# Four of eight pairs by seven products, five tiles summed by DMA, in both feed-forwards of a Conformer layer

## The chip, the cores and the metric

The kernel runs on one core of one Trainium2 chip. The metric is the time of one execution on the device in microseconds. Three runs of the kernel before took 2105.33, 2106.32 and 2113.24 us; their median is 2106.32 us. Where the text speaks of faster or slower, it compares such times of both kernels on the same chip.

## The reference, cut to what matters

One layer, 256 tokens of width 2048, all in float32:

```python
h = rms_norm(x, ffn1_norm);  x = x + 0.5 * swiglu_ffn(h, ffn1_w_in, ffn1_w_out)
h = rms_norm(x, mix_norm);   p = h @ w_mix_in        # conv value | conv gate | gMLP u | gMLP v
x = x + concat(rms_norm(conv_group(p)), rms_norm(gating_group(p))) @ w_mix_out
x = x + memory_cross_attention(rms_norm(x, xattn_norm), rms_norm(mem, mem_norm), w_q, w_kv, w_o)
h = rms_norm(x, ffn2_norm);  x = x + 0.5 * swiglu_ffn(h, ffn2_w_in, ffn2_w_out)
return rms_norm(x, final_norm)

def swiglu_ffn(h, w_in, w_out):
    gate, up = jnp.split(h @ w_in, 2, axis=-1)
    return (jax.nn.silu(gate) * up) @ w_out          # w_in 2048 x 11264, w_out 5632 x 2048
```

## The kernel before, in words

**Precision.** Every float32 operand is split into a high part, which is its value rounded to the type float32r, and a low part, the rest. A product of two matrices is three products of such parts: high by high, high by low, low by high. ScalarE makes the high part with a cast (L112 in most stages, L339 in the first half of a feed-forward), VectorE the low part with a subtraction (L113, L340). Weights come from DRAM as tiles of 128 x 1024 (512 KB) on SyncE's queue.

**The first half of a feed-forward** (class `FeedForward`, L299 to L513) computes silu(gate) * up. x lies with features on the partitions (`xT`), 16 tiles k of 128 features by 256 tokens, multiplied by the norm's gain (`gained`), split, and kept as `x_hl`. The inverse root of the mean square comes later, as a factor for each token, in `give`. The columns of `w_in` go in 11 groups of 512 gate and 512 up columns. Group 0 (`run`, the loop over k) is done plainly, 12 products of 128x512 for each k (`by_two`). For groups 1 to 10 the sixteen k go in eight pairs, and a string names how each is done:

- a C pair (`eight`) takes 2 x 12 = 24 products of 128x512;
- an S pair (`seven`) treats the two k tiles and the two token halves as a 2x2 block matrix and needs seven block products in place of eight, 21 products of 128x512. VectorE makes the sums of weight blocks (L388, L389, L394, L401), 512 columns each, and ScalarE and VectorE split four tiles, three of 1024 columns and one of 512. The matching sums of x (`forms`) are made once, by `sides`, during group 0.

The seven results lie in PSUM banks. After the last S pair (`spairs[-1]`) ScalarE copies one bank and VectorE combines it with three others (L439 to L443), which frees them; the C pairs go on adding to four banks, which are added at the group's end (L452), before `give` takes the silu. A group uses all eight banks, so that the next group's first products wait for these steps.

**Summed tiles.** For the k in `SUMMED` no low part is made on VectorE. `summed` has ScalarE write -w, rounded (L358), and the high part (L359) into a buffer of `hls`, and GpSimd's queue issues a DMA that adds w to -w in place (L360), which leaves the low part. When such a tile has been used, the next in order with the same buffer is begun.

**Buffers.** Split tiles go round in a ring: three of pool `whl` and two of `ring`. In the first feed-forward `x_given` adds one more to the ring, and a second buffer to `hls`, in the space of `xT`, since x is not needed in SBUF until the feed-forward's output is added; x is loaded from its input again later (L557 to L559). In the second, x is a result and stays in SBUF, so there is no such room. Weight tiles before the split go round in nine buffers, four of `wraw` and five of spare space.

**The second half** (`gemm_n`) multiplies the transposed result by `w_out`; the transposes (`turn`) run between its steps, the first four in the last group of the first half. In the second feed-forward x is transposed on VectorE (L989) into `x2` at the same time, for the final sum. At the end `add_up` and `give` (L1014 to L1042) make the final norm, first of one half of the tokens, then of the other.

**The start.** x, the vectors `pv` and the weights are loaded by SyncE's queue in program order; `x_squares` loads x a second time, tokens on the partitions, into tiles of `wraw` for the sums of squares.

**Order.** A planner puts each engine's instructions in an order before the run, by its own estimate of when each can start; on the chip each engine follows this order strictly. `issue_after` adds an edge to that order.

## Time and profile before

| | us |
|---|---|
| median of three runs | 2106.32 |
| the profiled execution | 2108.84 |
| its span, first to last instruction | 2107.0 |
| TensorE busy | 2084.5 |
| VectorE busy | 1576.8 |
| ScalarE busy | 1161.6 |

The profiled execution is a run of its own, with 1.84 us around its span. A matmul's busy time in the rows is its time from start to end; products overlap in the pipeline, so that the distance between starts is shorter than the row's duration. "L339" is a line of the kernel's source, "hl<-spare" a written tile and what is read. A row of a timeline has the start, the duration, the engine, the line, the operation, the tiles, the count and, in brackets, the idle time before it and what ended that. A row of groups has busy time, mean duration, idle time before and what ended most of it. The granted clock of TensorE was 0.998 on average.

### The profile page before, as it was taken

How to read it: one execution, taken by the hardware profiler on the slowest of the kernel's cores; microseconds unless marked ns; L12 is line 12 of the kernel's file. 1: busy time of each engine (PE TensorE's matmuls, PEld its weight loads, DVE VectorE, ACT ScalarE, POOL GpSimd, SP SyncE). 2: the span in 40 equal slices, each digit the busy share in tenths (PEclk: the TensorE clock that was granted, in tenths of full speed). 3: DMA queues.
4: the chain of work that ended last, by engine and by line, in shares of the span. 5: the costliest groups of instructions: out<-in, count | busy, mean ns of one | idle time of the engine just before them, and what ended most of it. 6: DMA issues, size and time to landing. Idle time of an engine off the chain costs nothing.

```text
span 2107.0 us, 26590 instructions
## 1 busy us (share of the span) xinstructions
PE 2084.5 (99%) x9764; PEld 1738.5 (83%) x9764; DVE 1576.8 (75%) x2215; ACT 1161.6 (55%) x1450; POOL 67.7 (3%) x83
## 2 busy tenths in 40 slices
PE   8999999999999999999999999999999999999998
PEld 6888888888888888888888888888888888888886
DVE  6888888876655589889877665777888887787754
ACT  7666566645544454445665454556665666554443
POOL 0000000000000000000000000000000000000000
PEclk9999999999999999999999999999999999999999
DMA  9778777855666676666565543686787778556664
GB/s 360 230 227 257 229 238 245 263 167 169 216 198 188 206 236 200 190 176 185 176 201 185 186 154 111 206 281 191 231 259 247 232 229 250 178 160 202 197 192 149
DMA packets 122244, 442.34 MB, mean 210 GB/s; under 512 B 13697, under 2 KB 13825, under 8 KB 121729
## 3 DMA queue, kind: packets, MB, share of 16 engines
q1 hardware_dynamic: 113184, 407.35, 58.8%
q0 software_dynamic: 8640, 32.51, 8.5%
q8 instruction: 76, 1.25, 0.2%
q10 hardware_dynamic: 288, 0.79, 0.1%
q14 instruction: 56, 0.45, 0.1%
HBM read 438.49 MB, written 2.10 MB: 209 GB/s over the span
## 4 chain that ended last, share of the span: by engine, by line
PE 84%; issue 11%; DMA 2%; ACT 1%; POOL 1%; DVE 1%; SPq 0%; POOLq 0%; ACTq 0%
PE acc L172 12%; PE acc L173 12%; PE acc L171 12%; PE acc L125 9%; PE acc L289 7%; PE acc L288 7%; PE acc L291 7%; PE acc L126 4%; PE acc L277 2%; PE acc L276 2%; PE acc L275 2%; PE aux L263 1%; PE acc L1066 1%; PE acc L1065 1%; PE acc L1067 1%
## 5 line engine op out<-in xcount | busy, mean ns | idle before, releaser
L113 DVE TENSOR_TENSOR hl<-raw,hl 128x1024 fp32r<-128x1024 f32 (+1 forms) x402 | 488.6, 1216 | 282.5 <-ACT hl L112 281.1
L112 ACT CAST hl<-raw 128x1024 fp32r<-128x1024 f32 (+1 forms) x402 | 419.7, 1045 | 481.6 <-PE acc L173 289.3
L339 ACT CAST hl<-spare 128x1024 fp32r<-128x1024 f32 (+1 forms) x135 | 131.8, 993 | 95.5 <-DVE spare L389 38.5
L340 DVE TENSOR_TENSOR hl<-spare,hl 128x1024 fp32r<-128x1024 f32 (+1 forms) x135 | 154.4, 1150 | 35.8 <-ACT hl L339 34.2
L288 PE MATMUL acc<-hl,x_hl 128*128 128x512 f32 x408 | 144.2, 394 | 9.7 <-ACT hl L339 9.7
L289 PE MATMUL acc<-hl,x_hl 128*128 128x512 f32 x408 | 149.9, 395 | 0.0
L340 DVE TENSOR_TENSOR hl<-raw,hl 128x1024 fp32r<-128x1024 f32 (+1 forms) x101 | 113.9, 1131 | 45.9 <-ACT hl L339 44.3
L339 ACT CAST ring<-spare 128x1024 fp32r<-128x1024 f32 (+1 forms) x99 | 97.2, 988 | 68.9 <-DVE spare L389 26.9
L340 DVE TENSOR_TENSOR ring<-spare,ring 128x1024 fp32r<-128x1024 f32 (+1 forms) x99 | 112.9, 1145 | 19.9 <-ACT ring L339 18.8
L291 PE MATMUL acc<-hl,x_hl 128*128 128x512 f32 x408 | 127.5, 392 | 0.0
L339 ACT CAST hl<-raw 128x1024 fp32r<-128x1024 f32 (+1 forms) x101 | 97.7, 977 | 51.8 <-PE acc L291 16.1
L172 PE MATMUL acc<-hl,x_hl 128*128 128x512 f32 x256 | 100.5, 392 | 0.2 <-DVE hl L113 0.2
L172 PE MATMUL acc<-hl,m_hl 128*128 128x512 f32 x256 | 100.4, 392 | 0.0
L173 PE MATMUL acc<-hl,m_hl 128*128 128x512 f32 x256 | 100.2, 391 | 0.0
L173 PE MATMUL acc<-hl,x_hl 128*128 128x512 f32 x256 | 99.8, 390 | 0.0
L288 PEld LDWEIGHTS acc<-hl,x_hl 128*128 128x128 f32 x408 | 76.8, 189 | 25.9 <-ACT hl L339 10.1
L289 PE MATMUL acc<-ring,x_hl 128*128 128x512 f32 x248 | 93.1, 389 | 0.0
L288 PE MATMUL acc<-ring,x_hl 128*128 128x512 f32 x248 | 91.2, 390 | 0.0
L171 PE MATMUL acc<-hl,m_hl 128*128 128x512 f32 x256 | 91.2, 393 | 0.0
L289 PEld LDWEIGHTS acc<-hl,x_hl 128*128 128x128 f32 x408 | 77.2, 190 | 16.9 <-DVE hl L340 1.1
L291 PEld LDWEIGHTS acc<-hl,x_hl 128*128 128x128 f32 x408 | 77.5, 190 | 16.4
L125 PE MATMUL acc<-x_hl,hl 128*128 128x512 f32 x256 | 91.0, 398 | 0.0
(359 smaller groups left out, 5173.9 us busy)
## 6 DMA issues: line engine op xcount, KB each, us to landing
spare<-in_ffn_w_in SPq DMA_DIRECT2D x192, 512.0 KB, 6.4
raw<-in_ffn_w_out SPq DMA_DIRECT2D x176, 512.0 KB, 3.8
raw<-in_ffn_w_in SPq DMA_DIRECT2D x160, 512.0 KB, 6.3
hl_s<-in_ffn_w_in POOLq DMA_DIRECT2D x44, 512.0 KB, 7.3
raw<-in_w_mix_vg SPq DMA_DIRECT2D x32, 512.0 KB, 4.6
raw<-in_w_k SPq DMA_DIRECT2D x32, 512.0 KB, 4.0
raw<-in_w_v SPq DMA_DIRECT2D x32, 512.0 KB, 4.4
raw<-in_w_mix_out SPq DMA_DIRECT2D x32, 512.0 KB, 4.6
```

Of the source, the lines that this page charges most:

```text
L112: nc.scalar.copy(out=hl[:, 0, :size], in_=raw[:, :size])
L113: newest[0] = nc.vector.tensor_tensor(out=hl[:, 1, :size], in0=raw[:, :size], in1=hl[:, 0, :size].bitcast(F32), op=ALU.subtract)
L125: nc.tensor.matmul(acc, lhsT=w_hi, rhs=x_hl, start=first, stop=False, skip_group_check=True)
L126: nc.tensor.matmul(acc[:, 0], lhsT=w_lo, rhs=x_hl[:, 0], start=False, stop=last, skip_group_check=True)
L171: nc.tensor.matmul(acc[t], lhsT=x[:, 0, s], rhs=hi[:, k], start=k0 + k == 0, stop=False)
L172: nc.tensor.matmul(acc[t], lhsT=x[:, 0, s], rhs=lo[:, k], start=False, stop=False)
L173: nc.tensor.matmul(acc[t], lhsT=x[:, 1, s], rhs=hi[:, k], start=False, stop=k0 + k == nk - 1)
L288: nc.tensor.matmul(acc[t][g], lhsT=x[:, 0, s], rhs=hi[:, cols[g]], start=(t, g) in first, stop=False)
L289: nc.tensor.matmul(acc[t][g], lhsT=x[:, 0, s], rhs=lo[:, cols[g]], start=False, stop=False)
L291: nc.tensor.matmul(acc[t][g], lhsT=x[:, 1, s], rhs=hi[:, cols[g]], start=False, stop=last)
L339: nc.scalar.copy(out=hl[:, 0, :n], in_=raw[:, :n])
L340: newest[0] = nc.vector.tensor_tensor(out=hl[:, 1, :n], in0=raw[:, :n], in1=hl[:, 0, :n].bitcast(F32), op=ALU.subtract)
```

## The change

- **Pairs.** Pair 6 turns from C to S in both patterns. The summed k go from 2, 7, 13 to 2, 6, 7, 11, 14. `sides` makes a fourth set of sums of x, at k = 15 of group 0. Two transposes rather than four run in the last group of the first half.
- **Space of x.** In the second feed-forward the residual x is stored to a DRAM tile (`kept`) while the attention's output product makes it, by four DMAs on GpSimd's queue; `x_given` then takes its space as in the first feed-forward, and `x_back` loads it again after the last group.
- **Head.** Gains and the first tile of x come as one transfer on ScalarE's queue, the second tile of x behind it. Eleven products of a tile of ones run on TensorE ahead of the first real one. The first weight tile comes and is split in two halves (`early`). The loads of x for the squares go to tiles of `h`, not `wraw`, and are asked for at k = 2, 4, 6, 8, not 5, 7, 9, 11. `give` of group 0 comes ahead of the second summed tile.
- **End.** Of the four partial sums of squares of the final norm, the first three are added, scaled and given the epsilon ahead of the last product (`most`); the last one goes directly into the square root. One operation with two factors from memory becomes a `tensor_scalar`.

```diff
-PATTERNS = ("SCSCSCCC", "SCSCSCCC")
-SUMMED = ((2, 7, 13), (2, 7, 13))
+PATTERNS = ("SCSCSCSC", "SCSCSCSC")
+SUMMED = ((2, 6, 7, 11, 14), (2, 6, 7, 11, 14))
+WARM = 11
...
-    xT = xt.tile([P, KD, T], F32, name="xT", tag="x")
+    gx = xt.tile([P, KD + KD * T], F32, name="gx", tag="x")
+    gains, xT = gx[:, :KD], gx[:, KD:].rearrange("p (k t) -> p k t", t=T)
+    nc.scalar.dma_start(out=gx[:, :KD + T], in_=a["gains_x0"])
+    nc.scalar.dma_start(out=xT[:, 1], in_=a["xT"][:, 1])
+    nc.vector.memset(ones, 1.0)
+    idle = pa.tile([P, 2, T], F32, name="aux")
+    for _ in range(WARM):
+        nc.tensor.matmul(idle[:, 0, :P], lhsT=ones, rhs=ones, start=True, stop=True)
...
+    def x_given():
+        more = xt.tile([P, 4, 1024], F32R, name="more", tag="x")
+        ff.ring.append(more[:, :2])
+        ff.hls.append(more[:, 2:])
+
+    def x_back(src):
+        xT = xt.tile([P, KD, T], F32, name="xT", tag="x")
+        for k in range(0, KD, 8):
+            nc.gpsimd.dma_start(out=xT[:, k:k + 8], in_=src[:, k:k + 8])
+        return xT
...
                     late = p > self.spairs[-1] and len(after) > 0
                     self.eight(j, p, b, p == self.pattern.index("C"), p == n - 1, late)
-                    if p > self.spairs[-1] + 1:
+                    if p >= n - 2:
...
+        def early(self, before):
+            self.raw_at += 1
+            self.at += 1
+            raw = wraw.tile([P, 1024], F32, name="raw")
+            hl = whl.tile([P, 2, 1024], F32R, name="hl")
+            halves = [slice(G, 2 * G), slice(0, G)]
+            for s in halves:
+                nc.sync.dma_start(out=raw[:, s], in_=self.w_in[0, :, 0, s])
+            x = before(0)
+            for s in halves:
+                with tc.issue_after(x.ins):
+                    split(hl[:, 0, s], hl[:, 1, s], raw[:, s])
+            return hl
...
+            self.give(0, [acc[t][0] for t in range(2)], [acc[t][1] for t in range(2)], r)
             if more is not None:
                 more()
                 self.summed(1)
-            self.give(0, [acc[t][0] for t in range(2)], [acc[t][1] for t in range(2)], r)
...
-                    now, turns = turns[:4], turns[4:]
+                    at = 2 * self.pattern[-2:].count("C")
+                    now, turns = turns[:at], turns[at:]
...
     def x_squares(c):
-        raw = wraw.tile([P, 1024], F32, name="raw")
+        raw = ff.h[7 - c].rearrange("p a b -> p (a b)")
...
-            if k in (5, 7, 9, 11):
-                x_squares(k // 2 - 2)
-            if k in (6, 9, 12):
+            if k in (2, 4, 6, 8):
+                x_squares(k // 2 - 1)
+            if k in (6, 9, 12, 15):
                 ff.sides(k // 3 - 2)
...
+            kept = tc.dram_tile([P, KD, T], F32, name="kept")
             for f in range(KD):
...
                 residual(acc, f, 1.0, x_hl, "ffn2_norm", ss)
+                if f % 4 == 3:
+                    nc.gpsimd.dma_start(out=kept[:, f - 3:f + 1], in_=xT[:, f - 3:f + 1])
...
-        turns = ff.run(lambda k: None, first_beside, lambda: rms_cols(ss, D, "r_x2"))
+        turns = ff.run(lambda k: None, first_beside, lambda: rms_cols(ss, D, "r_x2"), x_given)
+        xT = x_back(kept)
...
-            nc.vector.reduce_sum(out=tot, in_=sums[:, t], axis=AX.X)
-            nc.scalar.activation(out=s, in_=tot, func=AF.Sqrt, scale=1.0 / D, bias=eps)
-            nc.vector.tensor_scalar(out=v, in0=tot, scalar1=1.0 / D, scalar2=RMS_EPS, op0=ALU.mult, op1=ALU.add)
+            last = sums[:, t, 3:4]
+            nc.scalar.activation(out=s, in_=last, func=AF.Sqrt, scale=1.0 / D, bias=most[t])
+            nc.vector.tensor_scalar(out=v, in0=last, scalar1=1.0 / D, scalar2=most[t], op0=ALU.mult, op1=ALU.add)
             nc.vector.reciprocal(out=r, in_=s)
-            nc.vector.scalar_tensor_tensor(out=r, in0=v, scalar=r, in1=s, op0=ALU.mult, op1=ALU.add)
+            nc.vector.tensor_scalar(out=r, in0=v, scalar1=r, scalar2=s, op0=ALU.mult, op1=ALU.add)
...
+        most = [st.tile([P, 1], F32, name=f"f_most{t}") for t in range(2)]
+        for t in range(2):
+            nc.vector.reduce_sum(out=most[t], in_=sums[:, t, 0:3], axis=AX.X)
+            nc.vector.tensor_scalar(
+                out=most[t], in0=most[t], scalar1=1.0 / D, scalar2=RMS_EPS, op0=ALU.mult, op1=ALU.add
+            )
```

51 lines of the change are left out of this document (22 added, 29 removed).

## The prediction

> **What bounds the kernel now.** I read the page first, then the busy time of stretches, then single engines in order of time. The page's head, its busy line and the queue of GpSimd's transfers:
>
> ```profile
> span 2107.0 us, 26590 instructions
> PE 2084.5 (99%) x9764; PEld 1738.5 (83%) x9764; DVE 1576.8 (75%) x2215; ACT 1161.6 (55%) x1450; POOL 67.7 (3%) x83
> q0 software_dynamic: 8640, 32.51, 8.5%
> ```
>
> TensorE is busy in 99% of the span, so a product that goes away shortens the run, unless TensorE then waits for something. Stretches next: the start, the stretch after a late wait at 44.8, and one of about a column group in each feed-forward (busy time and count by engine, granted clock, DMA share, GB/s):
>
> ```profile
> core 0: us, PE busy (x) PEld busy (x) DVE busy (x) ACT busy (x) POOL busy (x), PEclk, DMA share, GB/s
> 7.10:12.00 4.90, 4.89 (x13) 3.89 (x14) 4.41 (x6) 3.83 (x6) 0.00 (x0) 1.00 1.02 369
> 44.80:49.40 4.60, 4.58 (x13) 3.34 (x14) 3.65 (x7) 2.40 (x3) 0.00 (x0) 0.63 1.04 315
> 101.00:143.00 42.00, 42.00 (x187) 34.80 (x186) 34.98 (x43) 25.59 (x30) 2.60 (x3) 1.00 0.75 241
> 1524.00:1566.00 42.00, 42.00 (x187) 34.80 (x186) 35.89 (x45) 26.48 (x29) 2.60 (x3) 1.00 0.79 239
> ```
>
> Inside the groups TensorE never rests, VectorE is busy 83 to 85%, ScalarE 61 to 63%, the DMA engines 75 to 79%. VectorE and the DMA engines are what the change can push to the edge.
>
> **The products.** TensorE's pitch, from product starts in one seven-product pair of the second feed-forward:
>
> ```profile
> 1524.37 0.39 PE L275 MATMUL acc<-ring 128*128 128x512 f32 x1
> ...
> 1526.86 0.39 PE L277 MATMUL acc<-hl,x_hl 128*128 128x512 f32 x1
> ```
>
> Eleven products lie between these starts: 2.49 / 11 = 0.226 us each. A C pair issues 24 of them, an S pair 21. One of eight pairs turns from C to S in ten groups of two feed-forwards: 20 x 3 = 60 products, **-13.6 us**. A group goes from 183 products, 41.4 us, to 180, 40.8 us.
>
> What this asks of the other engines, from the groups of instructions of the first feed-forward (us busy, mean ns | idle before):
>
> ```profile
> L340 DVE TENSOR_TENSOR hl<-spare,hl 128x1024 fp32r<-128x1024 f32 x48 | 58.2, 1222 | 8.0 <-ACT hl L339 7.4
> L388 DVE TENSOR_TENSOR spare<-spare 128x512 f32<-128x512 f32 x16 | 11.0, 686 | 10.1 <-DMA spare<-in_ffn_w_in 10.1
> L339 ACT CAST hl<-raw 128x1024 fp32r<-128x1024 f32 x33 | 34.4, 1050 | 8.2 <-PE acc L291 4.5 <-issue 1.4 <-PE aux L277 1.2
> ```
>
> VectorE: an S pair costs three wide splits and five half-wide operations, 3 x 1.22 + 5 x 0.69 = 7.1 us. Gone are the splits of k 12, 6, 11 and 14 (13 was summed already), 4 x 1.22 = 4.9. Net +2.2 on about 34.5 a group: 36.7 of 40.8, 90%. ScalarE: three wide casts and a half one (estimated 0.6) in, four casts out, two more summed tiles in, with two passes each, as long as a cast: +3.8 on 25.7, 72%. DMA: 8.5% of the span is 179 us for 8640 packets, or 2.65 for the 128 packets of a 512 KB tile, and five rather than three such tiles a group: +5.3 on 0.77 x 41.4 = 31.9, which makes 37.2 of 40.8, **91%**. None is over 100%, so none of them sets the pace by its sum; a wait must come from a latency or a burst.
>
> **The summed tiles** have the latency. Before a buffer can be used again, ScalarE writes -w into it, GpSimd issues the adding transfer, and it lands. A short turn in the second feed-forward, which has one buffer, and the landings of the same tile in the second and the first feed-forward, with who waited in the second:
>
> ```profile
> 1521.19 0.61 PE L291 MATMUL acc<-hl_s,x_hl 128*128 128x512 f32 x2
> ...
> 1530.71 0.39 PE L288 MATMUL acc<-hl_s,x_hl 128*128 128x512 f32 x1
> ```
> ```profile
> 1522.86 0.89 POOL L360 DMA_DIRECT2D hl_s<-in_ffn_w_in  x1 [11.50 <-ACT hl_s L358]
> ```
> ```profile
>   PE acc L289: 1.0, 2
> ...
> DMA to landing us min/median/max: 6.5/7.3/9.4
> ```
> ```profile
> DMA to landing us min/median/max: 5.3/8.1/9.8
> ```
>
> From the last use's end (1521.80) to the issue 1.06, to the next use 8.91: a landing of up to 7.85 costs nothing. At 7.3 it just fits, and only 1.0 us was lost. Afterwards both feed-forwards have two buffers but five tiles, k = 2, 6, 7, 11, 14. The same buffer serves 2 and 7, then 6 and 11: between the two uses lie one S pair and two k of C, as in the turn above (nearly 10 us by program order, less where the order moved products up). The other turns have a whole pair more. If 7 comes late by w, the turn from 6 to 11 is longer by w, so one wait a group is paid, not two. With the DMA engines at 91% I put landings above the 8.1 median, at 8.2: 0.35 us late, 20 groups, **+7 us**. Bounds: zero (6.5), and 0.85 at both turns of each group at a landing of 8.7, 34 us.
> The Trainium skill ("DMA: Bandwidth & Descriptors", section "Anatomy of one DMA — SWDGE (gpsimd) path") fits such a transfer at 2.0 us plus bytes over 436 GB/s, by which 512 KB would land in 3.2 us and this term would be nothing; the trace differs, with no landing under 5.3, and the sum goes by the trace.
>
> **The group's end.** Only one C pair, 5.4 us, follows the last S pair, not three. In it VectorE has four combinations (L440 to L443, of L388's size: 4 x 0.69 = 2.8), one split (1.2) and the first sums and split of the next group (2 x 0.69 + 1.22 = 2.6): 6.6. If nothing is done ahead, 1.2 us a group is late, as the next group's first bank is freed by the last combination; queued behind it are the next group's splits. Six tiles for splits (the second feed-forward gains one) let one split be ahead, which is enough. I take 0.05 us a group, **+1**; bounds 0 and 23 (20 groups).
>
> **x in DRAM.** Four 512 KB stores go out during the output projection and two 1 MB loads come back in the second feed-forward:
>
> ```profile
> L989 DVE STREAM_TRANSPOSE spare<-xT x128: 292/303/309, 1844.3 to 2015.7; 32x128 f32<-32x128 f32 x128
> ```
> ```profile
> xT<-in_xT POOLq DMA_DIRECT2D x2, 1024.0 KB, 6.4
> ```
>
> The first load can start once the last S pair has read its tiles, now 5.4 us ahead of the group's end, and lands about 1 us past it; the transposes began 1844.3, some 4 us ahead of that end. VectorE works in order, so a transpose placed too early would hold the splits behind it: 0 to 5 us, once. I take **+1**, which also covers that two rather than four turnings run ahead of the output product.
>
> **The head.** TensorE and ScalarE at the start and at the late wait:
>
> ```profile
> 7.11 2.07 PE L288 MATMUL acc<-hl,x_hl 128*128 128x512 f32 x4 [7.11 <-ACT hl L339]
> ...
> 11.96 1.07 PE L288 MATMUL acc<-hl,x_hl 128*128 128x512 f32 x4
> ...
> 44.82 1.50 PE L288 MATMUL acc<-hl,x_hl 128*128 128x512 f32 x4 [2.58 <-ACT hl L339]
> ...
> 49.34 0.39 PE L288 MATMUL acc<-ring,x_hl 128*128 128x512 f32 x1
> ...
> 59.07 0.50 PE L275 MATMUL acc<-hl,x_hl 128*128 128x512 f32 x1 [0.47 <-ACT h L418]
> ```
> ```profile
> 10.26 1.04 ACT L339 CAST hl<-raw 128x1024 fp32r<-128x1024 f32 x1 [0.39 <-DMA raw<-in_ffn_w_in]
> ...
> 42.69 1.06 ACT L525 ACTIVATE raw<-raw 128x1024 f32<-128x1024 f32 x1 [1.92 <-DMA raw<-in_x]
> ```
>
> The first twelve products take 4.85 us, not 2.72: a slow clock, though the clock column says 1.00 there. With eleven products on ones ahead and a smaller first transfer, the start is earlier and at speed, until it meets the weights: the third split (k = 2) is cast at 10.26 to 11.30, so k = 2 starts near 11.35, not 11.96 + 12 x 0.226 = 14.68: **-3.3**. At 44.82 TensorE waits for a split queued behind a late square of x, whose tile took a weight slot; this costs 2.6, and 4.52 instead of 2.72 for the next twelve products (granted clock 0.63), 1.8 more. x now has tiles of its own and is asked for earlier: **-4.4**. The silu at 59.07 goes ahead of the second summed tile's steps: **-0.5**. Against it: the DMA engines are full here (1.02), and each 512 KB of x asked for earlier pushes a weight back. A weight and its share of x, 640 KB, at 369 GB/s take 1.8 us against 2.7 us of products, and four x tiles in eight steps add 0.7 a step: 2.5, just inside. If it does not hold, the wait moves forward and only 3.3 is won.
> The Trainium skill ("TensorE: Matmul & The Clock Gate", section "What's actually happening") puts the slow clock back after about 3.4 us without work; by that the 2.6 us wait would not have cost clock and 1.8 of the gain would be absent. Granted 0.63 right after the wait speaks against it, and the sum stays with the row.
>
> **The tail.** VectorE's last steps for the first half of the tokens:
>
> ```profile
> 2095.60 0.16 DVE L1025 TENSOR_REDUCE f_tot<-sums 128x1 f32<-128x4 f32 x1 [0.79 <-ACT sq L1019]
> ...
> 2096.32 0.64 DVE L1029 SCALAR_TENSOR_TENSOR f_r<-f_v,f_r,f_s 128x1 f32<-128x1 f32 x1
> ```
>
> The reduction leaves the chain (0.2 with its hand-over), and the second step, another operation on one column, costs between the reduction's 0.16 and its present 0.64: 0.2 to 0.7 less for each half, both on the chain: **-0.8**.
>
> **Sum:** -13.6 - 8.2 - 0.8 + 7 + 1 + 1 = -13.6 against the profiled execution's 2108.84 (span 2107.0 and 1.84 around it): 2095.2. The runs' median, 2106.32, lies 2.5 lower, so the forecast for the runs is **2092.7**.
>
> **Rivals.**
> 1. *Nothing waits.* Landings stay at 7.3, since two buffers give the long turns room. The 1.0 us of waits now speaks for it, 91% against it. Gain 22.6: 2083.7.
> 2. *VectorE sets the group's end*, 1.2 us in 20 groups, the other waits hidden in these: 2106.3 - 22.6 + 23 = 2106.7. For it: the 6.6 us in 5.4; against: 10% idle and six tiles.
> 3. *The head gives only its start*: full DMA engines make a weight late where x is moved up. 2092.7 + 4.9 = 2097.6.
> 4. *Slower: the summed tile is late at both turns of every group.* Place: the first product on the summed tile at k = 7 and k = 11. Price: at a landing of 8.7, 0.85 x 40 = 34 us, at 9.0 46 us; then 2106.3 - 22.6 + 34 to 46 = 2117.7 to 2129.7. It decides from 0.57 us a turn, a landing of 8.4, where all is eaten. For it: 8.1 median and 9.8 at 75% load; against: a late k = 7 lengthens the next turn.
>
> **Chances.** A difference under 0.5%, 10.5 us, can hardly be told from none: faster is under 2095.8, slower over 2116.9. Forecast (2087 to 2099) 0.46, of it 0.38 under 2095.8; rival 1 0.17; rival 2 0.14; rival 3 0.14, of it 0.03 faster; rival 4 0.09, all slower. Faster 0.58, same 0.33, slower 0.09. Range 2083 to 2110: from no waits past rival 2, leaving out rival 4 and a little on the lower side.
>
> **What would show it.** Sixty fewer 128x512 products at 0.226; first k = 2 product near 11.4 and no wait near 44.8; two casts more a summed tile; a DMA share of 0.9 and VectorE at 0.9 in a group; waits of TensorE on the summed tiles of about 7 us in all; waits at the first products of a group near nothing. I am wrong if these waits pass 20 us, or if weights come late ahead of 40 us.

## The result, and the profile after

The kernel after takes 2197.22 us (median of six runs, 2189.12 to 2203.60), the one before on the same chip 2106.68 us: a ratio of 1.043, 95% interval 1.0414 to 1.0446. The forecast was 2092.7 us, with a range of 2083 to 2110; the kernel is 90 us slower. The profiled execution took 2203.6 us. Its page:

```profile
span 2201.8 us, 26741 instructions
PE 2125.9 (97%) x9726; PEld 1747.1 (79%) x9726; DVE 1613.1 (73%) x2307; ACT 1221.0 (55%) x1537; POOL 104.7 (5%) x129
q0 software_dynamic: 15264, 57.68, 13.8%
```

VectorE's and ScalarE's shares are no higher than before, the queue of GpSimd's transfers went from 8.5% to 13.8%, and TensorE's share fell from 99% to 97%. What TensorE waited for in the whole span (us in total, times, longest):

```profile
PE acc L303 <- DMA more<-in_ffn_w_in: 26.1, 11, 4.0
PE acc L303 <- DMA hl_s<-in_ffn_w_in: 23.3, 12, 5.5
PE acc L289 <- DVE spare L478: 8.6, 6, 6.2
PE aux L289 <- DVE spare L468: 3.0, 3, 1.4
```

49.4 us are waits on summed tiles (23 waits; 15 of them, 41.1 us, at k = 7); 11.6 are waits on VectorE's sums around a group's end. Three stretches of about a group, as before, and the 3.5 us behind one wait (busy time by engine, granted clock, DMA share, GB/s):

```profile
core 0: us, PE busy (x) PEld busy (x) DVE busy (x) ACT busy (x) POOL busy (x), PEclk, DMA share, GB/s
116.70:120.20 3.50, 3.50 (x8) 2.81 (x9) 1.21 (x2) 0.53 (x1) 0.00 (x0) 0.50 1.04 341
101.00:143.00 42.00, 38.88 (x157) 31.05 (x156) 31.15 (x39) 25.19 (x29) 4.36 (x5) 0.92 0.75 215
185.00:227.00 42.00, 40.63 (x174) 32.13 (x173) 35.25 (x46) 27.73 (x32) 3.49 (x4) 1.00 0.87 247
1524.00:1566.00 42.00, 38.42 (x155) 30.69 (x155) 28.95 (x37) 25.93 (x29) 4.35 (x5) 0.92 0.82 225
```

In 42 us TensorE issues 155 to 174 products, not 187. VectorE (69 to 84%) is no fuller than before, the DMA engines (75 to 87% against 75 to 79%) are a little fuller; by these averages neither is the bound. Averages hide bursts: in the 3.5 us behind the wait the DMA engines are full (1.04). One turn of a summed buffer, from the last product on its low part to the next one:

```profile
106.23 0.39 PE L303 MATMUL acc<-more,x_hl 128*128 128x512 f32 x1
...
106.66 1.06 ACT L384 ACTIVATE more<-raw 128x1024 fp32r<-128x1024 f32 x1 [2.62 <-PE acc L303]
...
108.14 0.88 POOL L386 DMA_DIRECT2D more<-in_ffn_w_in  x1 [14.97 <-ACT more L384]
...
113.19 0.40 PE L302 MATMUL acc<-more,x_hl 128*128 128x512 f32 x1
...
116.70 1.22 PE L303 MATMUL acc<-more,x_hl 128*128 128x512 f32 x2 [3.12 <-DMA more<-in_ffn_w_in]
117.72 1.05 PE L305 MATMUL acc<-more,x_hl 128*128 128x512 f32 x2
118.58 1.05 PE L303 MATMUL acc<-more,x_hl 128*128 128x512 f32 x2
```

ScalarE begins at once, GpSimd issues 1.48 us later, and the transfer takes 8.5 us (108.14 to about 116.66), little more than the 8.2 that was forecast. But TensorE came for the low part after 113.19, 6.8 us after it had left it. Then it waits 3.1 us, and two products behind the wait take 0.86 us (117.72 to 118.58), half speed.

**The account.** I took the distance from the start of each 128x512 product to the next start, over the whole trace, and set it against 0.2267 us. "Waits" are excesses over 0.3 us with a releaser, "half speed" is 0.15 us or more without one, "longer" under 0.06 us each.

| us | waits | half speed | longer products |
|---|---|---|---|
| before | 5.0 | 4.2 | 10.7 |
| after | 70.4 | 26.6 | 28.6 |
| difference | +65.4 | +22.4 | +17.9 |

With 13.6 us fewer products that is +92.1 of the +94.8 us by which the spans differ. The waits and the longer products got experiments of their own; the half speed follows waits (last section).

### The profile page after: what moved, and what is told of

Read it like the earlier page. It is cut to its first block, busy times and chain, and to the rows that moved or that the text cites. A ratio compares the mean times of both kernels' runs of the same rounds, so it can differ in the third digit from the quotient of the medians.

```text
span 2201.8 us, 26741 instructions
## 1 busy us (share of the span) xinstructions
PE 2125.9 (97%) x9726; PEld 1747.1 (79%) x9726; DVE 1613.1 (73%) x2307; ACT 1221.0 (55%) x1537; POOL 104.7 (5%) x129
## 3 DMA queue, kind: packets, MB, share of 16 engines
q0 software_dynamic: 15264, 57.68, 13.8%
q10 hardware_dynamic: 576, 1.06, 0.1%
## 4 chain that ended last, share of the span: by engine, by line
PE 60%; issue 33%; POOL 3%; DMA 2%; DVE 1%; ACT 1%; POOLq 0%; DVEq 0%; ACTq 0%
PE acc L176 12%; PE acc L175 12%; PE acc L174 12%; PE acc L128 8%; PE acc L129 4%; PE acc L303 2%; PE acc L305 2%; PE acc L302 2%; POOL hl_s L386 2%; POOL more L386 2%; PE aux L277 1%; PE acc L1108 1%; PE acc L1109 1%; PE acc L1110 1%; DMA more<-in_ffn_w_in 1%
## 5 line engine op out<-in xcount | busy, mean ns | idle before, releaser
L116 DVE TENSOR_TENSOR hl<-raw,hl 128x1024 fp32r<-128x1024 f32 (+1 forms) x402 | 489.2, 1218 | 285.0 <-ACT hl L115 284.0
L115 ACT CAST hl<-raw 128x1024 fp32r<-128x1024 f32 (+1 forms) x402 | 419.3, 1045 | 496.6 <-PE acc L176 306.4
L366 DVE TENSOR_TENSOR hl<-spare,hl 128x1024 fp32r<-128x1024 f32 (+1 forms) x126 | 143.6, 1145 | 63.5 <-ACT hl L365 63.5
L303 PE MATMUL acc<-more,x_hl 128*128 128x512 f32 x240 | 93.8, 421 | 26.1 <-DMA more<-in_ffn_w_in 26.1
L366 DVE TENSOR_TENSOR hl<-raw,hl 128x1024 fp32r<-128x1024 f32 (+1 forms) x85 | 91.5, 1084 | 17.9 <-ACT hl L365 17.5
L175 PE MATMUL acc<-hl,x_hl 128*128 128x512 f32 x256 | 100.4, 392 | 0.0
L176 PE MATMUL acc<-hl,x_hl 128*128 128x512 f32 x256 | 99.9, 390 | 0.0
L303 PE MATMUL acc<-hl_s,x_hl 128*128 128x512 f32 x200 | 77.0, 411 | 23.4 <-DMA hl_s<-in_ffn_w_in 23.3
L365 ACT CAST hl<-raw 128x1024 fp32r<-128x1024 f32 (+1 forms) x85 | 78.0, 937 | 37.0 <-DVE raw L427 25.0
L128 PE MATMUL acc<-y_hl,hl 128*128 128x512 f32 x256 | 90.5, 399 | 0.0
L128 PE MATMUL acc<-o_hl,hl 128*128 128x512 f32 x256 | 90.4, 399 | 0.0
L174 PE MATMUL acc<-hl,x_hl 128*128 128x512 f32 x256 | 90.1, 392 | 0.0
L175 PE MATMUL acc<-hl,hA 128*128 128x512 f32 x224 | 88.1, 393 | 0.0
L305 PE MATMUL acc<-more,x_hl 128*128 128x512 f32 x240 | 87.4, 415 | 0.0
L175 PE MATMUL acc<-hl,hB 128*128 128x512 f32 x224 | 87.4, 390 | 0.0
```

Source lines behind the costliest of these rows:

```text
L115: nc.scalar.copy(out=hl[:, 0, :size], in_=raw[:, :size])
L116: newest[0] = nc.vector.tensor_tensor(out=hl[:, 1, :size], in0=raw[:, :size], in1=hl[:, 0, :size].bitcast(F32), op=ALU.subtract)
L128: nc.tensor.matmul(acc, lhsT=w_hi, rhs=x_hl, start=first, stop=False, skip_group_check=True)
L174: nc.tensor.matmul(acc[t], lhsT=x[:, 0, s], rhs=hi[:, k], start=k0 + k == 0, stop=False)
L175: nc.tensor.matmul(acc[t], lhsT=x[:, 0, s], rhs=lo[:, k], start=False, stop=False)
L176: nc.tensor.matmul(acc[t], lhsT=x[:, 1, s], rhs=hi[:, k], start=False, stop=k0 + k == nk - 1)
```

## The experiments

Theory A: two summed buffers are too few. Theory B: the one C pair behind the last S pair is too short for VectorE. Theory C: a summed tile's weights hold one of nine weight buffers while ScalarE waits for the summed buffer, and SP's queue stands behind. Theory D: some operands of products lie at places in SBUF that make the products longer. Theory F: the DMA engines are full. Theory T: some turns of the summed buffers are too short. Ratios are to the kernel before on the same chip, in brackets the 95% interval.

**Old pairs and sums, new head and ends.** The counterpart of the kernel after without its main part.

```diff
-PATTERNS = ("SCSCSCSC", "SCSCSCSC")
-SUMMED = ((2, 6, 7, 11, 14), (2, 6, 7, 11, 14))
+PATTERNS = ("SCSCSCCC", "SCSCSCCC")
+SUMMED = ((2, 7, 13), (2, 7, 13))
-            if k in (6, 9, 12, 15):
+            if k in (6, 9, 12):
```

> The changed kernel with the pairs and the summed k of before (SCSCSCCC; 2, 7, 13), so that only the head, the end, the order of group 0's steps and the second feed-forward's x in DRAM with its extra buffers are left of the change. Theory A (the loss is TensorE waiting for summed tiles whose buffer comes round too soon) and theory B (the loss comes from the end of each group, where VectorE has only one C pair's time for the combinations) agree here: no loss, and the gain of head and end stands alone, 8.2 + 0.8 us: about 2097.5, within 2 us; the groups of both feed-forwards take 41.5 us each. If it comes out near 2107 or above, head and end gave nothing; over 2120 the x in DRAM is at fault, not the pairs.

2114.33 us, 1.0031 [1.0019, 1.0043]. In the table's terms TensorE waits 1.5 us in all and 0.8 are half speed. So the pairs and sums cost 83 us, and waiting comes with them. But it is 17 us over what was expected; the table's third column is 24.7 us here.

**Three sums with four S pairs**

```diff
-SUMMED = ((2, 6, 7, 11, 14), (2, 6, 7, 11, 14))
+SUMMED = ((2, 7, 14), (2, 7, 14))
```

> The changed kernel with three summed k a group (2, 7, 14) in place of five; four S pairs as in the change. VectorE has two wide splits more a group, 39 of 40.8 us. Theory A: two buffers for three tiles leave every turn at least 17 us, the waits on summed tiles go, and VectorE near its limit gives some waits back: 2095 to 2120. Theory B: VectorE is fuller at the end of the group than in the change: 2200 or more.

**Five sums with the old pairs** (the first edit without its change of sums; tiles 2, 6, 7, 11, 14).

> The changed kernel with the pairs of before (SCSCSCCC) and the new five summed k. VectorE is less loaded than in the kernel before, and three C pairs follow the last S pair. Theory A: the same buffer serves k = 2 and 7, then 6 and 11, as in the change, so TensorE waits for summed tiles there: 30 to 60 us of waits and as much again at a slow clock, 2150 to 2200. Theory B: no wait at the group's end, so no loss: 2095 to 2100.

Three sums, four S pairs: 2129.09 us, 1.0103 [1.0087, 1.0119]. Five sums, old pairs: 2171.3 us, 1.0303 [1.0281, 1.0325]. Two more sums cost 57 us with the old pairs and 68 with the new ones (2197.2 - 2129.1); the fourth S pair costs 15 with three sums and 26 with five. Theory B alone falls: with three C pairs at the group's end the five sums cost nearly as much. But theory A doesn't explain all of it either. The time with three sums lies above its forecast, though TensorE waits on no summed tile there: it waits 24 us, mostly on VectorE's sums, on casts and on splits. With five sums and the old pairs the time lies in its range, yet the largest wait is for VectorE's sums at the group's end, without a short last C pair:

```profile
PE acc L289 <- DVE spare L478: 19.6, 7, 4.8
PE acc L303 <- DMA hl_s<-in_ffn_w_in: 8.3, 7, 2.1
PE acc L303 <- DMA more<-in_ffn_w_in: 8.2, 8, 1.9
```

**A third summed buffer**, taken from the ring of split tiles.

```diff
-        ff.ring.append(more[:, :2])
+        ff.hls.append(more[:, :2])
...
                 more()
                 self.summed(1)
+                self.summed(2)
```

> The changed kernel with one edit: the second half of the space of x also goes to the summed tiles, which makes three buffers for them, and the ring for split tiles goes back from six to five. A buffer then comes round after three uses, not two. Theory A: the waits of TensorE on summed tiles (53 us in the changed kernel's profile) fall under 8 us and most of the slow clock behind them goes too (some 35 us): 2197 - 53 - 35 = 2109, or less. Theory B: the end of the group is as it was, and a smaller ring makes it worse: 2190 or more, with waits on banks in place of waits on summed tiles.

2206.12 us, 1.0471 [1.0449, 1.0494]. The waits on summed tiles fell from 49.4 us to 7.1, as theory A has it, and nothing was won; all waits together are some 72 us, and the time is in theory B's range:

```profile
PE aux L289 <- DVE spare L468: 11.6, 7, 3.6
PE acc L289 <- ACT ring L365: 10.5, 4, 4.4
PE acc L289 <- DVE spare L478: 10.2, 5, 3.2
PE acc L290 <- DVE ring L366: 6.7, 7, 1.8
PE acc L303 <- DMA more<-in_ffn_w_in: 4.6, 5, 1.9
...
PE acc L303 <- DMA hl_s<-in_ffn_w_in: 2.5, 3, 1.2
```

They moved to VectorE's sums, casts and splits. The ring has one tile less here, so that this edit can't say whether late weights or the shorter ring did it.

**Sums spread evenly.** Four at 2, 6, 10, 14 with four S pairs, and five at 2, 6, 10, 12, 15 with the old pairs.

```diff
-SUMMED = ((2, 6, 7, 11, 14), (2, 6, 7, 11, 14))
+SUMMED = ((2, 6, 10, 14), (2, 6, 10, 14))
```

> The kernel after with four summed tiles at 2, 6, 10 and 14 in place of five at 2, 6, 7, 11 and 14, so that a summed buffer has 17.7 us from its last product to its next one at every turn, where two of the five turns had 10.2 us. Theory T (the two short turns make the loss): the waits on summed tiles go from 24 us of a feed-forward to under 3, and the time is that of three sums or less, 2115 to 2130 us, though VectorE and the transfers have more to do than there. Rival (the work of five sums, on ScalarE, the queues or the transfers, is too much, so four is about half way): 2155 to 2170 us.

> The run with the old pairs and five sums, with these at 2, 6, 10, 12 and 15 in place of 2, 6, 7, 11 and 14: the same number of instructions and transfers, but one turn of 10.9 us and the others of 12.9 us and more, where two were of 10.2 us. Theory T: most of its loss against the three sums goes, 2120 to 2140 us. Rival (the amount of work): 2165 to 2175 us again.

2148.23 us, 1.0186 [1.0169, 1.0204], and 2160.81 us, 1.0253 [1.0239, 1.0268]. Both times lie between the two forecasts. The waits on summed tiles fell to 1.7 and 12.7 us in all, but much of the time stayed: of the 57 us for two more sums with the old pairs, 10 came back. To see how tight a turn is *as ordered*, I counted the products that stand in TensorE's order between the last one on a summed tile and the next one on the low part in the same buffer, times 0.2267 us; a turn needs some 9.4 us (1.46 from ScalarE's start to GpSimd's issue, a landing of 8.0 in the mean in the kernel after). The count beside the shortest turn is of turns under 8.5 us, about 1 us too short:

| kernel | turns | shortest, us | under 8.5 us | waits on summed tiles, us |
|---|---|---|---|---|
| before | 55 | 9.1 | 0 | 1.0 |
| after | 94 | 4.8 | 17 | 49.4 |
| old pairs, five sums | 94 | 6.6 | 2 | 16.5 |
| old pairs, five spread sums | 94 | 8.4 | 2 | 12.7 |
| four S pairs, four even sums | 74 | 8.8 | 0 | 1.7 |

Of the 17 short turns in the kernel after, 15 are those from k = 2 to k = 7. So theory T explains most of the waits on summed tiles in the kernel after, and these are most of its waits. With the old pairs and five sums 15 waits stand against 2 short turns; there landings of up to 13.2 us make turns late that are not short. It doesn't explain the spread kernel's other waits, 21 us of 33.7, on VectorE's sums and on casts and splits. VectorE itself waits for weights there (whole span; the spread kernel first, then the kernel before):

```profile
DVE spare L414 <- DMA raw<-in_ffn_w_in: 48.1, 16, 8.0
DVE spare L415 <- DMA spare<-in_ffn_w_in: 44.8, 15, 5.3
...
DVE spare L414 <- DMA spare<-in_ffn_w_in: 33.3, 16, 3.8
DVE spare L415 <- DMA raw<-in_ffn_w_in: 16.9, 12, 5.3
```
```profile
DVE spare L388 <- DMA spare<-in_ffn_w_in: 20.6, 10, 3.0
DVE spare L389 <- DMA raw<-in_ffn_w_in: 12.1, 7, 3.1
DVE spare L388 <- DMA raw<-in_ffn_w_in: 8.7, 8, 2.1
```

143 us against 41; in the kernel after it is 55. Theories F and C both make weights late.

**Half the added bytes**, in the spread kernel.

```diff
-            nc.gpsimd.dma_start(out=hl[:, 1], in_=self.w_in[j, :, k], accum_op=ALU.add)
+            nc.gpsimd.dma_start(out=hl[:, 1, :G], in_=self.w_in[j, :, k, :G], accum_op=ALU.add)
```

> The run with the old pairs and five spread sums (2160.8 us), whose adding transfers bring only the first 512 of 1024 columns: the second half of a summed tile's low part is left as minus the high part, so this kernel leaves out half of those additions. All instructions, waits and plain loads stay; only the transfers' time falls, from about 26 loads' worth a group to 21, below the 22 of the kernel before. Theory F (the transfers of five sums fill the engines: 38 us of a group of 41): the groups come to 42 to 42.5 us and the time to 2110 to 2125 us. Theory C (SP's queue stands behind a weight buffer that waits for ScalarE's step on a summed tile): only the 15 us of waits directly on summed tiles go, 2140 to 2155 us.

**More transfers**, in the run with the old pairs and 32 bytes put in (below).

```diff
             nc.gpsimd.dma_start(out=hl[:, 1], in_=self.w_in[j, :, k], accum_op=ALU.add)
+            nc.gpsimd.dma_start(out=self.beside[at % 8], in_=self.w_in[j, :, k])
```

> The run with the old pairs, three sums and 32 bytes put in (2106.7 us), with three more transfers a group: behind each adding transfer, POOL's queue copies the same 512 KB of weights from DRAM into DRAM, where nothing reads it. Nothing else is changed and nothing waits for it. If such a copy costs the engines as much as one to two loads, a group has 25 to 28 loads' worth, as with five sums. Theory F: slower by 25 us or more, 2130 to 2165 us, with casts and splits late. Theory C: within 5 us of the run without, 2104 to 2112 us.

Half the added bytes: 2153.53 us, 1.0215 [1.0197, 1.0232], 7 us less than the spread kernel, though the queue of the adding transfers went from 31.9% to 18.5% of the engines in the first feed-forward (130 to 450 us). The landings fell from 7.9 to 6.2 us in the mean and the waits on summed tiles to 2.5 us; VectorE still waited 121 us for weights. This is theory C's forecast, and theory F falls for the spread kernel; in the kernel after it was not tried, but the run with two buffers set apart (below), with the same transfers, speaks against it there.

The second run tells less than it was meant to: 2175.27 us, 1.0323 [1.0308, 1.0338], but nothing waits for the copies, and the planner put all of them at the start, so that they were issued in the first 145 us:

```profile
50.00:130.00 80.00, 56.80 (x211) 42.72 (x209) 37.20 (x48) 36.79 (x43) 17.77 (x32) 0.85 1.03 400
```

There the engines are really full (1.03, against 0.75 to 0.87 in the kernel after), TensorE issues 211 products where a later stretch of 80 us of this run has 354, and from the third group on all take 41.6 us again. It shows what DMA engines look like that are full over 80 us, and that the kernel after isn't there on average.

**Summed tiles' weights out of SP's queue.** Three attempts. First, in the kernel after with 32 bytes put in (below), one buffer of its own, loaded by GpSimd's queue:

```diff
-            raw, hl = self.raw(j, k), self.hls[at % len(self.hls)]
+            raw, hl = self.free_raw, self.hls[at % len(self.hls)]
+            nc.gpsimd.dma_start(out=raw, in_=self.w_in[j, :, k])
```

> The aligned kernel after, in which the weights of a summed tile are loaded by POOL's queue into one buffer of their own, and the other eight buffers turn among the remaining weights on SP's queue. Theory C (a summed tile's weights hold one of the nine buffers until ScalarE's step, and SP's queue stands behind it, so that the following weights, casts and splits are late): SP's waits for ScalarE's copy of a summed tile go from about 147 us of the first feed-forward to under 20, TensorE's waits behind casts and splits fall by half, and the time falls by 20 us or more against the aligned one (2150 to 2165 us). Rival (the turns of the two summed buffers themselves are too short, whatever the queue does): the waits on summed tiles stay, and the time is within 8 us of the aligned one, or longer, since eight buffers are left.

2256.76 us, 1.0705 [1.0675, 1.0735]. The load stands behind the adding transfer in the same queue, and ScalarE's step began 7 to 10 us late at many turns; waits on summed tiles rose to 68.5 us. Second, in the spread kernel, one buffer loaded by ScalarE's queue:

```diff
             nc.scalar.copy(out=hl[:, 0], in_=raw)
+            if at + 1 < len(self.sums_at):
+                nj, nk = self.sums_at[at + 1]
+                nc.scalar.dma_start(out=raw, in_=self.w_in[nj, :, nk])
```

> The run with the old pairs and five spread sums (2160.8 us), in which a summed tile's weights are loaded by ScalarE's queue into one buffer of their own, as soon as the step on the tile before it is done, and the other eight buffers turn among the remaining weights on SP's queue; the transfers are the same in number and size. Theory C: SP's waits for ScalarE's copies (124 us of the first feed-forward) go, and the time falls by 20 us or more, 2115 to 2140 us. Theory F: 2155 to 2170 us, since the same is moved.

2219.64 us, 1.0533 [1.0517, 1.055]. SP's waits for ScalarE's copies are gone and VectorE waits 16 us for weights instead of 143, which is theory C's part. But the time is above both forecasts: one buffer is too few; now ScalarE waits for the weights, with its casts behind it:

```profile
ACT hl_s L387 <- DMA spare<-in_ffn_w_in: 149.4, 43, 7.5
ACT more L387 <- DMA spare<-in_ffn_w_in: 141.9, 40, 6.8
```

Third, the kernel after with two of the nine buffers set apart, loaded two tiles ahead, and operands placed as in the kernel before:

```diff
-            self.raws = [spare[:, i * 1024:(i + 1) * 1024] for i in (5, 0, 1, 2, 3)]
+            self.raws = [spare[:, i * 1024:(i + 1) * 1024] for i in (5, 0, 1)]
+            self.own_raws = [spare[:, i * 1024:(i + 1) * 1024] for i in (2, 3)]
...
+        def ahead(self, at):
+            if at < len(self.sums_at):
+                j, k = self.sums_at[at]
+                nc.scalar.dma_start(out=self.own_raws[at % 2], in_=self.w_in[j, :, k])
...
             nc.scalar.copy(out=hl[:, 0], in_=raw)
+            self.ahead(at + 2)
```

> The kernel after (2197 us) with two of the nine weight buffers set apart for the weights of summed tiles, loaded by ScalarE's queue as soon as the step on the tile two before is done, and seven left to SP's queue, which has 11 loads a group in place of 16; every operand of a product lies where it lies in the kernel before. Number and size of the transfers are the same. Theory C (SP's queue, standing behind a summed tile's weights, makes the other weights late): SP's waits for ScalarE's copies, 147 us of the first feed-forward, go; VectorE's and ScalarE's waits for late weights fall under 10 us, and what is left are the two short turns a group, 0.3 us to spare at 10.2 us: 2100 to 2140 us. Rival (the short turns and the slow clock behind them make the loss by themselves): 2170 us or more, with as much waiting on summed tiles as in the kernel after (23 us and 29 us).

2138.2 us, 1.0152 [1.0133, 1.017]: 59 us of the 90 are back, with the same transfers and the DMA engines fuller (0.86 in 101 to 143 us). TensorE's largest waits now:

```profile
PE aux L288 <- DVE spare L475: 6.1, 4, 1.9
PE acc L288 <- DVE spare L485: 5.4, 5, 2.3
PE acc L175 <- DVE hl_s L123: 5.2, 2, 3.5
PE acc L301 <- ACT hl L365: 4.5, 1, 4.5
PE acc L302 <- DMA hl_s<-in_ffn_w_in: 3.2, 3, 2.2
PE acc L302 <- DMA more<-in_ffn_w_in: 2.9, 5, 0.9
```

In the table's terms 34.5 us of waits, 10.1 at half speed, 12.2 of longer products. Against the kernel after that is 52.4 us less of waits and half speed, and 16.4 less of longer products, since the operands lie elsewhere too; the places are a part of the 59. And there is a reservation on the rest: the planner knows the queues, and it wrote another order (562 of ScalarE's 1537 instructions are others at their place in the sequence). The shortest turn as ordered is 7.9 us instead of 4.8, and 2 instead of 17 are under 8.5. So this run takes away the blocked queue *and* most of the too short turns; it doesn't tell how much each gave. One sign speaks against late weights as the main cause: they were to cost VectorE and ScalarE under 10 us here, but VectorE waits 79 us for them, more than the 55 of the kernel after (ScalarE 15 instead of 46):

```profile
DVE spare L422 <- DMA raw<-in_ffn_w_in: 44.0, 20, 7.4
...
DVE spare L422 <- DMA spare<-in_ffn_w_in: 27.7, 11, 5.4
...
DVE spare L421 <- DMA raw<-in_ffn_w_in: 6.9, 8, 2.2
```

The last run adds even sums (2, 6, 10, 14) to it.

> The run before (two buffers set apart, loaded by ScalarE's queue, operands where the kernel before has them) with four sums at 2, 6, 10 and 14 in place of five, so that every turn of a summed buffer has 17.7 us. Theory C with the short turns as what was left: no waits on summed tiles, groups at 40.8 to 41.5 us, 2088 to 2108 us, which may beat the best so far (2099 us). Rival: with one sum less, VectorE has more splits to do (36 us of a group of 40.8) and sets the pace with the seven buffers of SP's queue: waits on the sums at a group's end and on splits, groups at 42 us and more, 2112 to 2130 us.

2120.57 us, 1.007 [1.005, 1.0089]; the time is the rival's, though the groups take 39.5 to 44.7 us, 41.6 on average, and not 42 and more. It is 28 us less than the run with the same sums without buffers set apart, but here too the operands were moved, and the longer products are 10.8 us instead of 26.4. Waits are 23.5 us, of which 4.5 are on summed tiles. In both runs some 6 us of waits lie in the head, where the new loads come between others.

**Places of operands.** In the kernel before the tiles of weight parts begin multiples of 8192 bytes from those of the x parts that they are multiplied with; inside the tiles the operands are steps of 512 bytes apart. The change takes one column out of a pool and puts the gains in front of x, so that the two summed buffers (`more`, `hl_s`) come to lie 32 bytes off. These runs only move tiles; the order of all instructions is the same as in the kernel that each is compared with. First, the kernel before without its 32 bytes of padding:

```diff
-    st.tile([P, 8], F32, name="to_64")
```

> The kernel before, with its 32 bytes of unused space taken out, so that its x, summed and h tiles begin 32 bytes past a multiple of 64; nothing else is changed. Theory D: products from the added buffers at 232 to 235 ns instead of 227, groups of the first feed-forward at about 42.0 us instead of 41.5, and 2110 to 2120 us. If the shift is of no matter: 2104 to 2109 us.

2116.37 us, 1.0048 [1.0033, 1.0064]: 9.7 us slower, and the longer products go from 10.7 us to 21.1. The first products on `hl_s` (duration least/median/most), before and shifted:

```profile
L288 PE MATMUL acc<-hl_s,x_hl x176: 387/389/402, 59.9 to 1825.5; 128*128 128x512 f32 x176
```
```profile
L287 PE MATMUL acc<-hl_s,x_hl x176: 392/395/399, 56.6 to 1830.7; 128*128 128x512 f32 x176
```

Then the kernel after, and the run with the old pairs, with 32 bytes more, which gives multiples of 64 again; the latter also with 64 bytes behind x, which puts `hl_s` 128 bytes off; and four even sums with both.

```diff
     st.tile([P, 8], F32, name="to_64")
+    st.tile([P, 8], F32, name="to_64_too")
```

> The kernel after, with 32 bytes a partition of unused space put in front of the x, second summed and h tiles, so that they begin at a multiple of 64 bytes again as in the kernel before. Theory D (the shifted start makes a product from the two added buffers 6 to 7 ns longer): pitch of those products back at 227 ns, some 0.5 us off each of 20 groups, 2180 to 2190 us. If the shift is of no matter: 2194 to 2200 us. Under both, the single waits on summed tiles and sums stay, since they are not of this cause.

> The head, the ends and x in DRAM with the pairs and the three sums of before (as in the run with the old pairs), with the 32 bytes put in. Theory D: groups at 41.5 us as in before and 2097 to 2102 us, which would be faster than the kernel before by 0.2 to 0.45 per cent. If the shift is of no matter: 2113 to 2116 us again.

```diff
-    gx = xt.tile([P, KD + KD * T], F32, name="gx", tag="x")
-    gains, xT = gx[:, :KD], gx[:, KD:].rearrange("p (k t) -> p k t", t=T)
+    gx = xt.tile([P, 2 * KD + KD * T], F32, name="gx", tag="x")
+    gains, xT = gx[:, :KD], gx[:, KD:KD + KD * T].rearrange("p (k t) -> p k t", t=T)
```

> The run with the old pairs and 32 bytes put in, with 64 bytes more behind x, so that the second summed and the h tiles too begin at the same place of a 128-byte line as the x and weight parts that they are multiplied with (in the run before, they began 64 bytes beside). If a product is longer wherever its two operands begin at different places of such a line: the products from hl_s and hC go from 231 to 234 ns to 227, and 5 us fall away, to 2099 to 2103 us, faster than before by 0.2 to 0.35 per cent. If it is another cause: 2105 to 2108 us again.

> The run with four summed tiles at 2, 6, 10 and 14, with all operands at the same place of a 128-byte line (32 bytes put in front of x, 64 behind it). By the groups of the run with old pairs this is worth 10 to 15 us where TensorE sets the pace: 2100 to 2118 us by theory T and the line rule together; where waits set the pace, as in the kernel after, it is worth nothing, as there.

Last, the run with the old pairs with each operand at the very place of the kernel before:

```diff
-    st.tile([P, 8], F32, name="to_64")
...
-    pv = const.tile([P, NPV], F32, name="pv")
+    pv = const.tile([P, NPV + 16], F32, name="pv")
...
-        more = xt.tile([P, 4, 1024], F32R, name="more", tag="x")
+        more = xt.tile([P, 16 + 4 * 1024], F32R, name="more", tag="x")[:, 16:].rearrange("p (a n) -> p a n", n=1024)
```

> The run with the old pairs, with every tile that holds an operand of a product at the very place that it has in the kernel before (64 unused bytes behind the columns of gains and biases, the 32 in front of x taken out, the added buffers 64 bytes into their space). If the length of a product hangs on the distance between its two operands, as in before all those distances are multiples of 8192 bytes: products from hl_s, hC and the added buffers at 227 ns, and 2099 to 2103 us, faster than before by 0.2 to 0.35 per cent. If not: 2105 to 2108 us.

| run | bytes off these multiples: `more`, `hl_s` | ns from start to start: `more`, `hl_s` | us | ratio |
|---|---|---|---|---|
| before | 0, 0 | 226.6, 226.9 | 2106.7 | |
| before, shifted | -32, -32 | 233.6, 233.6 | 2116.4 | 1.0048 |
| old pairs | -32, +32 | 233.5, 233.6 | 2114.3 | 1.0031 |
| old pairs, 32 bytes in | 0, +64 | 227.0, 231.2 | 2106.7 | 0.9999 [0.999, 1.0008] |
| old pairs, 32 and 64 in | 0, +128 | 226.8, 232.1 | 2106.3 | 0.9994 [0.9985, 1.0002] |
| old pairs, placed as before | 0, 0 | 226.7, 226.7 | 2099.0 | 0.996 [0.9946, 0.9975] |

Theory D holds, but neither for multiples of 64 nor of 128: 128 bytes off is still long; only tiles with no offset come to 227. Between the first and the last run with the old pairs lie 15.3 us. The last, with a median of 2098.99 us, is the fastest kernel here, 8 us under the kernel before.

Where TensorE waits anyway, the places are worth little: the kernel after with 32 bytes in takes 2198.18 us, 1.0432 [1.0418, 1.0446], as without; its products are some 6 us shorter in all and its waits some 6 us longer. Four even sums with both take 2144.4 us, 1.0178 [1.0151, 1.0204], 4 us less than without, which is inside the spread of either (2138.7 to 2153.1 and 2144.7 to 2158.1).

## Why the prediction was wrong, step by step

**The products** are gone as counted (9764 records before, 9726 after, of which 22 belong to the eleven products of ones: 60 fewer), but the 13.6 us never showed in a time. Even with three sums, where TensorE waits on no summed tile, the four S pairs made 2129 us of 2114. So a second step is in doubt, that TensorE busy in 99% of the span turns a product that goes away into time: waits that came with the pair took more than it gave, 24 us there. VectorE had more splits to do in that run than in the kernel after, so it doesn't tell the size for the kernel after.

**The summed tiles: this step failed.** It forecast 7 us, 0.35 in each of 20 groups; the waits are 49.4, and 20.9 us at half speed follow them. The mechanism and the place were right: 15 of the 20 groups wait at k = 7, and k = 11 costs only 5.2 us, so that mostly one wait a group is paid and not two, as forecast. The size was wrong: 2.7 us for each of the 15. The landing was right (8.2 forecast, 8.0 in the mean and 8.3 in the median). Wrong was the other side, the time allowed: "From the last use's end (1521.80) to the issue 1.06, to the next use 8.91: a landing of up to 7.85 costs nothing" was read from one turn of the kernel before and taken for all, with a hint that the order might move products up. It did: the turn from k = 2 to k = 7 has 6.5 us of products in the median of its 20 cases, 4.8 at the least, where 9.4 are needed. The single turn above shows it, 6.8 us where 10 are needed. The issue was not later than assumed: it comes 1.48 us after ScalarE's start in that turn, and 1.47 in the quoted one (1521.39 to 1522.86); the 1.06 counts from the end of the tile's last product.

In the same step the price of a wait was its length alone, though the same prediction quotes a row with a granted clock of 0.63 behind a wait. And what a summed tile holds besides its buffer was not costed: its weights. SP's waits for ScalarE's copies, in the kernel before (two rows) and after (two rows):

```profile
SPq L349 <- ACT hl_s L359: 130.0, 40, 9.4
SPq L349 <- ACT more L359: 17.2, 10, 9.1
```
```profile
SPq L375 <- ACT more L385: 182.9, 45, 9.8
SPq L375 <- ACT hl_s L385: 123.8, 40, 8.9
```

The 130 us before cost nothing, so the total of such a row proves nothing; the runs with buffers set apart are the evidence, and these don't separate the queue from the turns. What share of the loss the weights have stays open.

The Trainium skill's fit for such a transfer ("DMA: Bandwidth & Descriptors", "Anatomy of one DMA — SWDGE (gpsimd) path"), 3.2 us for 512 KB, would have made this term nothing; the traces differ, with 8.0 in the mean in the kernel after. To keep to the row was right and did not help.

**The group's end** was forecast at 1 us, bounds 0 and 23: the waits for VectorE's sums are 11.6 us in nine places. Right kind, size wrong; the short last C pair isn't needed for it, as the old pairs with five sums show (19.6 us). What makes VectorE late there was not tried.

**The engines' shares** were forecast at 0.9 each and stayed below, because a group lasts longer. That none is over 100% was true and no comfort.

**A term that was missing**: 17.9 us of longer products. The change moves tiles by 32 bytes; nothing in the prediction asked where they come to lie.

**The head** was nearly right: -8.2 forecast, -7.6 measured. The wait at 44.8 is gone, and the group's second product, which waited for the silu at 59.07, starts 7.6 us earlier:

```profile
5.77 0.78 PE L302 MATMUL acc<-hl,x_hl 128*128 128x512 f32 x1
...
11.80 1.07 PE L302 MATMUL acc<-hl,x_hl 128*128 128x512 f32 x4
...
51.46 0.50 PE L289 MATMUL acc<-hl,x_hl 128*128 128x512 f32 x1 [0.49 <-ACT h L444]
```

k = 2 begins at 11.80 (forecast 11.35), and the silu is still waited for, so that the 0.5 us for it did not come.

**The tail** was right: the step on one column takes 0.27 instead of 0.64 us, and the span ends 8.8 us after the last product's end (2193.0) where it was 10.0 (2097.0). **x in DRAM** costs nothing: from the end of the second feed-forward's first half to the last product's end it is 248.4 us in the run placed as before, 248.9 in the kernel before.

```profile
2192.00 0.27 DVE L1064 TENSOR_SCALAR f_r<-f_v,f_r,f_s 128x1 f32<-128x1 f32 x1
```

Head, tail and x in DRAM were forecast together at -8.0 us; the run placed as before, which has them alone, is 8 us under the kernel before.

**The rivals.** The slower one, both turns of every group late, came nearest and had 0.09. Of its two places, k = 7 holds 41.1 us and k = 11 holds 5.2; its 34 to 46 us stand against 49.4 us of waits, and without the half speed and the longer products it stops at 2129.7.

**Still open** is what the spread and the set-apart kernels have left, 20 to 30 us of waits on casts, splits and sums, and why the planner packs the turns as it does; neither was tried.

## What to carry to other kernels

Take the time that a latency may use from the order in which the changed kernel will issue its work, at every turn, not from one turn of the kernel before; an average share of 80% on each engine says nothing on it. A wait of TensorE of 2 us or more may cost 1.7 us beyond its length. When an edit changes what is allocated, look at the distance between the two operands of the products, and undo that first: here a change whose sound parts won 8 us measured as slower until the tiles were put back.

## What the runs showed of the hardware

**A product's length depends on where its operands lie to each other.** 226.7 ns from start to start where they lie a multiple of 512 bytes apart, 231 to 234 ns at 32, 64 or 128 bytes off it (table above), with the instructions in the same order. 256 bytes were not tried. The Trainium skill ("SBUF — State Buffer", section "SBUF: two separate sides") says that TensorE, on the engines' side of SBUF, never waits on anyone; no run here tests that. The cause of the longer products stays open: 3% of a product went with the places alone.

**When a wait costs clock.** In all 20 traces I took each wait (its excess over 0.2267 us) that follows at least 16 products at full speed, and the excess of the next twelve products:

| wait, us | waits | excess, mean | least to most |
|---|---|---|---|
| 0.5 to 1.75 | 148 | 0.18 | 0.12 to 0.49 |
| 1.75 to 2.25 | 38 | 0.59 | 0.13 to 1.74 |
| 2.25 to 3.25 | 28 | 1.10 | 0.12 to 1.75 |
| 3.25 to 4.9 | 6 | 1.72 | 1.70 to 1.73 |

Between 1.75 and 3.25 us it is the one or the other: 37 waits cost 0.20 us or less, 29 cost 1.30 or more, none between. The Trainium skill ("TensorE: Matmul & The Clock Gate", section "What's actually happening") has the slow clock after at least one idle window of about 3.4 us, the full clock after a busy one as long, and the window run freely; the traces agree above 3.25 us, and on how long the slow clock lasts (0.50 granted in the 3.5 us shown), but waits of 1.9 us already brought it.
